# Seven Winograd products of a decoder's mixer in another order, with half of the attention projection split in two

## The chip, the cores and the metric

One NeuronCore of a Trainium2 chip runs the whole program. The metric is the device time of one execution in microseconds; a time of a kernel is the median of several runs.

## What is computed

Two layers, each a mixer and an MLP on 512 tokens of width 1024, all in fp32. The parts that matter here, cut from the reference's description:

```
h = RMSNorm(x)
z = h @ W_in  (columns: attention q k v | mLSTM q k v | mLSTM o-gate | i/f logits | gates A, B)
branch A: causal sliding-window attention (8 heads of 64, window 128)
branch B: mLSTM matrix memory (4 heads), per-head RMS norm, sigmoid output gate
merged = sigmoid(gA) * (A @ W_att_branch) + sigmoid(gB) * (B @ W_m_branch)
x = x + merged @ W_out
x = x + relu(RMSNorm(x) @ W1)^2 @ W2
```

## The kernel before

**Arithmetic.** Each fp32 operand is split into a high and a low part (`split`, `chunk`, `parts_of`: a copy on ScalarE, L165 or L722, then a subtraction on VectorE, L166 or L723), and each product of two blocks is three matmuls (`mm3`, L47): high by high, high by low, low by high. A chunk is 128 rows of a weight, 512 columns wide: loaded into one of three raw buffers, split into one of four pairs of slots.

**What sets the order of a mixer.** The function `mixer` builds a list of steps of matmuls (the *fill*), each 0.25 of a unit, three matmuls; a unit is twelve. Beside it stands a list `side` of functions with a position in units. `weave` (L222) emits the fill in its order and calls each side function when the fill has come to its position. So the order of every engine's queue is written by hand, by these positions; only what stands in `high_priority` or behind `issue_after` is moved.

**The fill before:** the mLSTM q and k (8 units), the gates s0 and s1 (8 each), product 2, the attention branch's projection a in two halves of 512 columns (4 units each, four chunks each, four PSUM banks each), products 5, 1, 3, 6, 7, 4 (2 units each), the gates s2 and s3. There are five banks for all of these.

**The seven products** are a 2 by 2 Winograd form of the product with the columns V and O of W_in. Their second factors are sums of blocks of W_in: products 1 and 2 use a block as it is, through `chunk`; products 5, 6 and 4 use one raw block per k (`wa[k]`, four of them), which is loaded (`begin`, from SP's queue) and gets another block added by a DMA that accumulates (GpSimd's queue, L729); after product 5 has split it another is added (`more`, L717), and after product 6 another. Products 3 and 7 use `wb[k]` (`begin_other`, `more`) in the same way. Product 4 gives its own result, which is added on VectorE (L795) to a copy of product 7's (L793, ScalarE).

**Evacuation of a.** When a half of a is done in its four banks, `ev_a` multiplies each on VectorE with its gate (L915; L910 in the changed file).

**The m phase** (mLSTM) runs as side functions beside s2 and s3: per head `m_decay`, then per block of tokens `m_weights` and `m_out` (four matmuls into an aux bank, then a norm on ScalarE, L892 and L893, and the gate, `m_gate`, on VectorE, L899). After the last one `m_norm` turns the collected squares into factors (two activations with a table load each, L238 and L239, then VectorE L241 to L244), multiplies the four gated rows (L907) and `head_tr` transposes them head by head on TensorE (L52), for the projection of the m branch behind s3. `qk_split` (L674 to L682) readies the mLSTM q and k, with a cast on GpSimd (L676).

Of the kernel before, what the change touches and what calls it, by code (L numbers as in the profile page):

```python
# [12 lines left out]
AF = mybir.ActivationFunctionType  # L13
# [20 lines left out]
def hybrid_kernel(ctx, tc, x, norm_mix, w_in, att_q_norm, att_k_norm, att_sinks, m_gate_bias,  # L34
# [353 lines left out]
    def mixer(l, norm, late, order, phase):  # L388
# [8 lines left out]
        def wcols(c0, n):  # L397
            return lambda k: [W[k * P:(k + 1) * P, c0:c0 + n]]
# [146 lines left out]
        qT, sps, parts = {}, {}, {}  # L545
        tri_i = tri_l.bitcast(I32)

        def k_vec(b):
# [73 lines left out]
        def att_probs(b, kv):  # L622
            sp = sps[b, kv]
            pt = aux()
            for i in range(4):
                pe.transpose(pt[:, i * P:(i + 1) * P], sp[:, i * P:(i + 1) * P], ident)
            hl = split(pt, get=lambda: temp(F32R))
            parts[b, kv] = [(hl, v2[:, 0, max(b - 1, 0), kv])]
            if b > 0:


                own = [temp(F32R) for _ in hl]
                for src, dst in zip(hl, own):
                    s3, d3 = (t.rearrange("p (h q) -> p h q", h=4) for t in (src, dst))
                    gp.affine_select(out=d3, in_=s3, compare_op=ALU.is_ge, fill=0.0, base=0,
                                     pattern=[[0, 4], [1, P]], channel_multiplier=-1)
                parts[b, kv].append((own, v2[:, 1, b - 1, kv]))

        def att_out(b, kv):
# [86 lines left out]
        def begin(k):  # L726
            wa[k] = slot()
            load(wa[k], 0, 0, k)
            gp.dma_start(wa[k], block(0, 1, k), accum_op=ALU.add)  # L729

        def begin_other(k):
            wb[k] = slot()
            load(wb[k], 1, 1, k)
# [55 lines left out]

        def output(t, i, ps, first):  # L790
            if first:
                so.append(slot() if t else temp())
                sc.activation(so[-1], ps, AF.Copy)  # L793
            else:
                ve.tensor_tensor(so[2 * t + i], so[2 * t + i], ps, op=ALU.add)  # L795

        def gates_o():
            for b in range(NB):
                sc.activation(so[b], so[b], AF.Tanh, scale=half[:, b:b + 1])

        plan = {2: ("f", (0, 1), [(output, 0, True)]), 5: ("y", None, [(value, 1, True)]),
                1: ("x", (0, 0), [(output, 0, False)]), 3: ("y", None, [(value, 0, True)]),
                6: ("x", None, [(value, 0, False)]), 7: ("x", None, [(value, 1, False), (output, 1, True)]),
                4: ("f", (1, 1), [(output, 1, False)])}
        held, ready = {}, {}
        by_weights = [(k, i) for k in range(4) for i in range(2)]
        by_tokens = [(2 * h + k, i) for h in range(2) for i in range(2) for k in range(2)]

        def vo_step(n, k, i):
            which, at, outs = plan[n]  # L810
            fresh = n in (5, 1, 2, 4) and k == 0
            if fresh and i == 0:
                held[which] = [bank(), bank()]
            if i == 0:
                ready[k] = weight(n, k)
            wh, wl = ready[k]
            if at:
                c = slice(H * at[0] + i * P, H * at[0] + (i + 1) * P)
                ah, al = (a[:, c] for a in acts[4 * at[1] + k])
            else:  # L820
                ah, al = (a[:, k % 2, i * P:(i + 1) * P] for a in sums[n][k // 2])
            mm3(held[which][i], ah, al, wh, wl, fresh, False, skip_group_check=True)
            if k == 3:
                with tc.high_priority():
                    for f, t, first in outs:
                        f(t, i, held[which][i], first)

        def vo_steps(*ns):
            return [(0.25, lambda n=n, k=k, i=i: vo_step(n, k, i))
                    for n in ns for k, i in (by_tokens if n in (6, 7) else by_weights)]  # L830
# [4 lines left out]
        for i, (b, kv) in enumerate(units):  # L835
# [6 lines left out]
            if kv == 0 and b + 1 < NB:  # L842
                if b + 2 < NB:
                    side += [(at + 1, lambda b=b: k_vec(b + 2)), (at + 1, lambda b=b: q_vec(b + 2))]
                side += [(at + 2 * 1.65 - 1.75, lambda b=b: k_tr(b + 1)), (at + 2 * 1.65 - 2.15, lambda b=b: q_tr(b + 1))]
        side += [(8.45, gating0), (25.5, gating1), (30.5, gating2), (35.5, gating3)]
        side += [(at, lambda m=m, i=i: qk_split(m, i))
                 for at, m, i in ((37.0, 0, 0), (38.0, 2, 0), (39.5, 0, 1), (41.0, 2, 1),
                                  (43.5, 1, 0), (45.0, 3, 0), (46.5, 1, 1), (48.0, 3, 1))]
        g0, s0 = gate_steps(0)  # L850
        g1, s1 = gate_steps(1)

# [29 lines left out]
        def m_out(h, t):  # L882
            ps = aux([P, MV + 1])
            for s in range(t + 1):
                pe.matmul(ps, wts[h, s][:, (t - s) * P:(t - s + 1) * P], vm[0][:, s, h, :],
                          start=s == 0, stop=s == t)
            dn = sm([P, 1], "dn")
            ve.scalar_tensor_tensor(dn, ps[:, MV:], -1.0, em[:, t, h:h + 1], op0=ALU.mult, op1=ALU.max)
            ve.tensor_tensor(dn, ps[:, MV:], dn, op=ALU.max)
            ve.reciprocal(dn, dn)  # L890
            hs = hm[t][:, h * MV:(h + 1) * MV]
            sc.activation(hs, ps[:, :MV], AF.Copy, scale=dn)  # L892
            sc.activation(ps[:, :MV], hs, AF.Square, accum_out=hss[:, t, h:h + 1])  # L893
            if h > 1:
                m_gate(h, t)

        def m_gate(h, t):
            c = slice(h * MV, (h + 1) * MV)
            ve.scalar_tensor_tensor(hm[t][:, c], so[t][:, c], 1.0, hm[t][:, c], op0=ALU.add, op1=ALU.mult)  # L899

        def m_norm():
            ve.tensor_scalar(hss, hss, 1.0 / MV, EPS, op0=ALU.mult, op1=ALU.add)
# [5 lines left out]

        prod = []

        def a_steps(g, sg):
            def ev_a(m, ps):
                t = sg[m]
                prod.append(t)
                ve.scalar_tensor_tensor(t, t, 1.0, ps, op0=ALU.add, op1=ALU.mult)  # L915

            return feat_steps(att_acts, lambda k: [w_att_branch[l, k * P:(k + 1) * P, 512 * g:512 * g + 512]],
                              ev_a)
# [11 lines left out]
        side.append((49.1, gates_o))  # L930
        side += [(49.3 + 0.9 * h + 0.15 * t, lambda h=h, t=t: m_gate(h, t)) for h in range(2) for t in range(NB)]
# [569 lines left out]
```

## Time and profile before

| | |
|---|---|
| median of 3 runs | 1299.78 us (1298.21 to 1300.07) |
| the profiled execution | 1299.13 us |
| its span in the trace | 1297.4 us |
| TensorE | 1282.7 us busy, 99%, 6930 matmuls, clock 1.00 |
| VectorE, ScalarE, GpSimd | 1008.3 us (78%), 776.3 (60%), 236.2 (18%) |
| DMA, mean | 142 GB/s read from HBM over the span |

The first mixer's fill runs from about 61 to 260 us of the span, the second one's some 642 us later. In the rows, PE is TensorE, DVE VectorE, ACT ScalarE, POOL GpSimd, SP the queue that issues most loads. A row of a timeline has its start, its length, engine, line, operation and tiles; the brackets hold the engine's idle time just ahead and what ended it. Matmuls overlap, and their ends are modelled. `x4` is four instructions merged in one row.

### The profile page before, as it was taken

The numbers are of one execution on the slowest core, as the hardware profiler recorded it, in microseconds if no ns is written. First come the engines' busy times: TensorE is split into PE (matmuls) and PEld (weight loads), VectorE is DVE, ScalarE is ACT, GpSimd is POOL, SyncE is SP. The second block draws the span as 40 slices with busy tenths as digits, with TensorE's granted clock in tenths as the row PEclk, the third lists the DMA queues.
The fourth block names the chain that finished last, engine by engine and source line by source line (L and its number), as shares of the span: only waits on it lengthen the run. The fifth ranks groups of instructions, "written<-read, shape, count | busy, mean of one in ns | idle before, by whom it ended". The sixth has DMA issues, their size and how long they took to land.

```text
span 1297.4 us, 19218 instructions
## 1 busy us (share of the span) xinstructions
PE 1282.7 (99%) x6930; PEld 1095.2 (84%) x6930; DVE 1008.3 (78%) x1608; ACT 776.3 (60%) x1367; POOL 236.2 (18%) x313
## 2 busy tenths in 40 slices
PE   9999999999999999999999999999999999999998
PEld 6877778888889999999888777788888899999987
DVE  4688898674777897968958888876747879879797
ACT  5568578553465656656554785775435556665563
POOL 4501252000003021131114023310000030311210
PEclk9999999999999999999999999999999999999999
DMA  5422672272369888898224226722714597988953
GB/s 155 111 74 58 187 130 66 74 243 81 98 163 172 240 183 207 199 206 215 33 77 112 66 60 178 129 77 79 259 50 131 146 214 193 205 210 198 217 142 98
DMA packets 135151, 186.01 MB, mean 143 GB/s; under 512 B 10376, under 2 KB 78832, under 8 KB 135056
## 3 DMA queue, kind: packets, MB, share of 16 engines
q1 hardware_dynamic: 94208, 131.82, 33.2%
q0 software_dynamic: 40128, 52.57, 25.5%
q8 instruction: 54, 0.88, 0.3%
q10 hardware_dynamic: 720, 0.40, 0.1%
q14 instruction: 41, 0.34, 0.1%
HBM read 182.65 MB, written 2.10 MB: 142 GB/s over the span
## 4 chain that ended last, share of the span: by engine, by line
PE 91%; DVE 3%; DMA 3%; ACT 2%; issue 1%; DVEq 0%; SPq 0%; ACTq 0%
PE mm L47 73%; PE aux L47 16%; PE aux L52 2%; DMA w<-in_w_in_dram 2%; DMA w<-in_w_att_branch_dram 1%; ACT wh L165 1%; DVE wl L166 1%; ACT t L615 0%; DVE wl L723 0%; DVE t L583 0%; DVE a L915 0%; DMA x<-in_x_dram 0%; DVE t L620 0%; DVE m L609 0%; DVE t L176 0%
## 5 line engine op out<-in xcount | busy, mean ns | idle before, releaser
L47 PE MATMUL mm<-i,wh 128*128 128x512 f32 (+1 forms) x1280 | 353.9, 363 | 0.2
L992 ACT ACTIVATE wh<-raw 128x1024 fp32r<-128x1024 f32 x212 | 223.3, 1056 | 189.4 <-PE mm L47 118.6
L993 DVE TENSOR_TENSOR wl<-raw,wh 128x1024 fp32r<-128x1024 f32 x212 | 255.1, 1219 | 75.3 <-ACT wh L992 75.3
L47 PEld LDWEIGHTS mm<-i,wh 128*128 128x128 f32 x1280 | 222.7, 189 | 30.7 <-DVE a L695 1.1
L47 PE MATMUL mm<-i,wl 128*128 128x512 f32 (+1 forms) x640 | 228.8, 359 | 0.0
L166 DVE TENSOR_TENSOR wl<-w,wh 128x512 fp32r<-128x512 f32 (+1 forms) x192 | 129.0, 675 | 100.7 <-ACT wh L165 96.3
L165 ACT ACTIVATE wh<-w 128x512 fp32r<-128x512 f32 (+1 forms) x192 | 116.7, 610 | 113.8 <-PE mm L47 85.0
L47 PE MATMUL mm<-wh,uh 128*128 128x512 f32 x440 | 171.8, 390 | 0.0
L47 PE MATMUL mm<-wl,uh 128*128 128x512 f32 x440 | 171.7, 390 | 0.0
L47 PE MATMUL mm<-wh,ul 128*128 128x512 f32 x440 | 171.2, 389 | 0.0
L1152 POOL DMA_DIRECT2D raw<-in_w_ff_dram x48 | 62.2, 1303 | 543.0 <-DVE i L179 234.2
L47 PEld LDWEIGHTS mm<-i,wl 128*128 128x128 f32 x640 | 120.9, 189 | 18.5 <-DVE wl L993 0.4
L47 PE MATMUL mm<-wh,i 128*128 128x512 f32 (+1 forms) x352 | 101.3, 361 | 1.2 <-ACT wh L165 0.6
L1038 DVE SCALAR_TENSOR_TENSOR x<-mm,ms,x 128x512 f32<-128x512 f32 x126 | 90.5, 744 | 9.0 <-PE mm L47 8.9
L47 PEld LDWEIGHTS mm<-wh,ul 128*128 128x128 f32 x440 | 82.6, 188 | 17.5
L47 PEld LDWEIGHTS mm<-wh,uh 128*128 128x128 f32 x440 | 82.8, 188 | 16.1
L47 PEld LDWEIGHTS mm<-wl,uh 128*128 128x128 f32 x440 | 82.8, 188 | 15.6
L47 PE MATMUL mm<-a,wh 128*128 128x512 f32 x256 | 79.8, 393 | 2.3 <-DVE a L915 2.3
L47 PE MATMUL mm<-wh,a 128*128 128x512 f32 x256 | 81.4, 393 | 0.0
L47 PEld LDWEIGHTS mm<-wh,i 128*128 128x128 f32 x352 | 62.0, 188 | 12.4 <-DVE i L179 1.5
L1309 POOL DMA_DIRECT2D raw<-in_w_ff_dram x36 | 43.6, 1212 | 149.2 <-DVE wl L993 103.3
L47 PE MATMUL aux<-t,wh 128*128 128x256 f32 x384 | 69.5, 283 | 0.0
(284 smaller groups left out, 2409.3 us busy)
## 6 DMA issues: line engine op xcount, KB each, us to landing
raw<-in_w_ff_dram SPq DMA_DIRECT2D x144, 512.0 KB, 5.1
raw<-in_w_ff_dram POOLq DMA_DIRECT2D x84, 512.0 KB, 7.9
w<-in_w_in_dram SPq DMA_DIRECT2D x112, 256.0 KB, 2.7
a<-in_w_in_dram POOLq DMA_DIRECT2D x32, 256.0 KB, 5.9
w<-in_w_out_dram SPq DMA_DIRECT2D x32, 256.0 KB, 3.1
w<-in_w_att_branch_dram SPq DMA_DIRECT2D x16, 256.0 KB, 5.4
a<-in_w_in_dram SPq DMA_DIRECT2D x16, 256.0 KB, 5.5
w<-in_w_m_branch_dram SPq DMA_DIRECT2D x16, 256.0 KB, 2.7
```

What stands on the lines that cost most here:

```text
L47: latest[0] = nc.tensor.matmul(*args, **kw)
L52: latest[0] = nc.tensor.transpose(*args)
L165: sc.activation(wh[:, :off], raw[:, :off], AF.Copy)
L166: ve.tensor_tensor(wl[:, :off], raw[:, :off], f32(wh[:, :off]), op=ALU.subtract)
L992: sc.activation(hi, src, AF.Copy)
L993: ve.tensor_tensor(lo, src, f32(hi), op=ALU.subtract)
L1038: ve.scalar_tensor_tensor(xh[:, cc], ps[i][:, cc], ms[j][:, b:b + 1], xh[:, cc], op0=ALU.mult, op1=ALU.add)
L1152: gp.dma_start(to[h], src(h, i, j), accum_op=ALU.add)
L1309: gp.dma_start(to[h], src(h, i, j), accum_op=ALU.add)
```

## The change

The fill becomes: q and k, s0, s1, product 2, the first half of a (4 units, four banks), product 1, the first quarter of a (2 units, two banks), products 5, 6, 3, 7, the second quarter, product 4, s2, s3. Further:

- The eight loads of raw blocks are called at positions 17 to 21.8 where they were at 24.5 to 29.5; the four first accumulations are their own function and are issued behind the last mask of the attention on GpSimd.
- Product 4 goes on in the PSUM banks of products 1, 6 and 7 and gives the sum; its Tanh is taken straight from PSUM. The other gates' Tanh follow their add at once.
- Products 6 and 7 go by weight chunk rather than by pairs of chunks per half of the tokens.
- The m phase, the third gating and the q and k splits start half a unit to a unit and a half later, and the transposes of the heads half a unit; all gates of m are applied where the head's output is.

```diff
@@ vo products @@
         def begin(k):
             wa[k] = slot()
             load(wa[k], 0, 0, k)
-            gp.dma_start(wa[k], block(0, 1, k), accum_op=ALU.add)
+
+        def begin_sum(k):
+            with tc.issue_after(masked[0].ins):
+                gp.dma_start(wa[k], block(0, 1, k), accum_op=ALU.add)
...
             else:
-                ve.tensor_tensor(so[2 * t + i], so[2 * t + i], ps, op=ALU.add)
...
+                ve.tensor_tensor(so[i], so[i], ps, op=ALU.add)
+                sc.activation(so[i], so[i], AF.Tanh, scale=half[:, i:i + 1])
+
+        def output_whole(t, i, ps, first):
+            so.append(slot())
+            sc.activation(so[-1], ps, AF.Tanh, scale=half[:, 2 * t + i:2 * t + i + 1])
...
-        plan = {2: ("f", (0, 1), [(output, 0, True)]), 5: ("y", None, [(value, 1, True)]),
-                1: ("x", (0, 0), [(output, 0, False)]), 3: ("y", None, [(value, 0, True)]),
-                6: ("x", None, [(value, 0, False)]), 7: ("x", None, [(value, 1, False), (output, 1, True)]),
-                4: ("f", (1, 1), [(output, 1, False)])}
+        plan = {2: ("f", (0, 1), [(output, 0, True)]), 1: ("x", (0, 0), [(output, 0, False)]),
+                5: ("y", None, [(value, 1, True)]), 6: ("x", None, [(value, 0, True)]),
+                3: ("y", None, [(value, 0, False)]), 7: ("x", None, [(value, 1, False)]),
+                4: ("x", (1, 1), [(output_whole, 1, True)])}
...
-            fresh = n in (5, 1, 2, 4) and k == 0
+            fresh = n in (5, 1, 2) and k == 0
...
-        side += [(8.45, gating0), (25.5, gating1), (30.5, gating2), (35.5, gating3)]
+        side += [(8.45, gating0), (25.5, gating1), (30.5, gating2), (36.5, gating3)]
...
-                 for at, m, i in ((37.0, 0, 0), (38.0, 2, 0), (39.5, 0, 1), (41.0, 2, 1),
-                                  (43.5, 1, 0), (45.0, 3, 0), (46.5, 1, 1), (48.0, 3, 1))]
+                 for at, m, i in ((38.5, 0, 0), (39.5, 2, 0), (41.0, 0, 1), (42.0, 2, 1),
+                                  (44.5, 1, 0), (45.5, 3, 0), (47.0, 1, 1), (48.0, 3, 1))]
...
+        def a_half_steps(h):
...
+            ps, w = [], []
+
+            def step(q, m, i):
+                if q == 0 and m + i == 0:
+                    ps.extend((bank(), bank()))
+                if m + i == 0:
+                    w[:] = chunk([w_att_branch[l, k * P:(k + 1) * P, 512 + H * h:512 + H * (h + 1)]
+                                  for k in range(2 * q, 2 * q + 2)])
+                k, c = 2 * q + i, slice(H * i + m * P, H * i + (m + 1) * P)
+                mm3(ps[m], w[0][:, c], w[1][:, c], *att_acts[k], k == 0, k == 3)
+                if k == 3:
+                    with tc.high_priority():
+                        ev_a(g1[2 * h + m], ps[m])
...
-        side += [(24.5 + 0.5 * k, lambda k=k: begin(k)) for k in range(4)]
-        side += [(28.0 + 0.5 * k, lambda k=k: begin_other(k)) for k in range(4)]
-        side += [(27.0, sums1), (31.0, lambda: sums_next(6, 0, 0)), (33.5, lambda: sums_next(3, 0, 1)), (38.0, sums3)]
+        side += [(17.0 + 0.6 * k, lambda k=k: begin(k)) for k in range(4)]
+        side += [(20.0 + 0.6 * k, lambda k=k: begin_other(k)) for k in range(4)]
+        side += [(24.6 + 0.3 * k, lambda k=k: begin_sum(k)) for k in range(4)]
+        side += [(27.0, sums1), (31.0, lambda: sums_next(6, 0, 0)), (33.5, lambda: sums_next(3, 0, 1)),
+                 (36.5, sums3)]
...
-            at = 39.6 + pace * h
+            at = 40.6 + pace * h
...
-        side.append((56.9, m_norm))
+        side.append((57.9, m_norm))
...
-        side += [(59.6 + 0.75 * f, lambda f=f: head_tr(f)) for f in range(MH)]
-        weave(feat_steps(acts, wcols(C_QM, 512), ev_qk) + s0 + s1 + vo_steps(2) + a_steps(0, g0) + a_steps(1, g1)
-              + vo_steps(5, 1, 3, 6, 7, 4) + s2 + s3, side)
+        side += [(60.1 + 0.75 * f, lambda f=f: head_tr(f)) for f in range(MH)]
+        weave(feat_steps(acts, wcols(C_QM, 512), ev_qk) + s0 + s1 + vo_steps(2) + a_steps()
+              + vo_steps(1) + a_half_steps(0) + vo_steps(5, 6, 3, 7) + a_half_steps(1) + vo_steps(4)
+              + s2 + s3, side)
```

Three places of the first mixer, in the order of the engines' queues. **SP's queue** around the loads of a's weights (`w<-in_w_att_branch`); the raw blocks are the rows at L713. Before:

```order
L155 DMA w_1805<-in_w_att_branch_dram 128x512
L155 DMA w_1839<-in_w_att_branch_dram 128x512
L713 DMA a_1732<-in_w_in_dram 128x512
L155 DMA w_1859<-in_w_att_branch_dram 128x512
L713 DMA a_1747<-in_w_in_dram 128x512
L713 DMA a_1782<-in_w_in_dram 128x512
L713 DMA a_1801<-in_w_in_dram 128x512
L155 DMA w_1881<-in_w_att_branch_dram 128x512
L155 DMA w_1906<-in_w_att_branch_dram 128x512
L155 DMA w_1951<-in_w_att_branch_dram 128x512
L713 DMA a_1857<-in_w_in_dram 128x512
L713 DMA a_1871<-in_w_in_dram 128x512
```

After, from the last raw block on:

```order
L713 DMA a_1643<-in_w_in_dram 128x512
L155 DMA w_1748<-in_w_in_dram 128x512
L155 DMA w_1762<-in_w_in_dram 128x512
L155 DMA w_1796<-in_w_in_dram 128x512
L155 DMA w_1813<-in_w_att_branch_dram 128x512
L155 DMA w_1847<-in_w_att_branch_dram 128x512
L155 DMA w_1865<-in_w_att_branch_dram 128x512
L155 DMA w_1883<-in_w_att_branch_dram 128x512
L155 DMA w_1907<-in_w_in_dram 128x512
L155 DMA w_1933<-in_w_in_dram 128x512
L155 DMA w_1955<-in_w_in_dram 128x512
L155 DMA w_1967<-in_w_in_dram 128x512
```

All eight raw blocks have left the place among the weights of a, and behind a's first four weights come those of product 1 (`in_w_in`).

**TensorE's queue** at the end of a's first half, before (the first three rows are its last chunk into its fourth bank; `a` as first operand are gated attention rows):

```order
L47 MATMUL mm_1822<-a_635,wh_1883 128x512
L47 MATMUL mm_1822<-a_636,wh_1883 128x512
L47 MATMUL mm_1822<-a_635,wl_1884 128x512
L47 MATMUL mm_1905<-a_629,wh_1908 128x512
L47 MATMUL mm_1905<-a_630,wh_1908 128x512
L47 MATMUL mm_1905<-a_629,wl_1909 128x512
L47 MATMUL mm_1915<-a_629,wh_1908 128x512
L47 MATMUL mm_1915<-a_630,wh_1908 128x512
L47 MATMUL mm_1915<-a_629,wl_1909 128x512
```

After, at the same row numbers:

```order
L47 MATMUL mm_1830<-a_635,wh_1885 128x512
L47 MATMUL mm_1830<-a_636,wh_1885 128x512
L47 MATMUL mm_1830<-a_635,wl_1886 128x512
L47 MATMUL mm_1905<-wh_1909,i_114 128x512
L47 MATMUL mm_1905<-wl_1910,i_114 128x512
L47 MATMUL mm_1905<-wh_1909,i_115 128x512
L47 MATMUL mm_1906<-wh_1909,i_114 128x512
L47 MATMUL mm_1906<-wl_1910,i_114 128x512
L47 MATMUL mm_1906<-wh_1909,i_115 128x512
```

Behind the first half stands product 1 (in its rows the weight stands first and the tokens, `i`, second) with two banks, where the second half of a stood, with four.

**TensorE's queue** at the first head's transposes (L52; `a_170` to `a_173` are the gated rows of the four blocks of tokens, the matmuls around them are s3). Before:

```order
L47 MATMUL mm_2837<-i_274,wh_2970 128x512
L47 MATMUL mm_2837<-i_275,wh_2970 128x512
L47 MATMUL mm_2837<-i_274,wl_2971 128x512
L47 MATMUL mm_2841<-i_274,wh_2970 128x512
L47 MATMUL mm_2841<-i_275,wh_2970 128x512
L47 MATMUL mm_2841<-i_274,wl_2971 128x512
L52 MATMUL aux_2983<-ident,a_170 128x128
L52 MATMUL aux_2983<-ident,a_171 128x128
L52 MATMUL aux_2983<-ident,a_172 128x128
L52 MATMUL aux_2983<-ident,a_173 128x128
L47 MATMUL mm_2855<-i_274,wh_2970 128x512
L47 MATMUL mm_2855<-i_275,wh_2970 128x512
```

After:

```order
L47 MATMUL mm_2834<-i_274,wh_2968 128x512
L47 MATMUL mm_2834<-i_275,wh_2968 128x512
L47 MATMUL mm_2834<-i_274,wl_2969 128x512
L47 MATMUL mm_2796<-i_274,wh_2986 128x512
L47 MATMUL mm_2796<-i_275,wh_2986 128x512
L47 MATMUL mm_2796<-i_274,wl_2987 128x512
L52 MATMUL aux_2993<-ident,a_170 128x128
L52 MATMUL aux_2993<-ident,a_171 128x128
L52 MATMUL aux_2993<-ident,a_172 128x128
L52 MATMUL aux_2993<-ident,a_173 128x128
L47 MATMUL mm_2818<-i_274,wh_2986 128x512
L47 MATMUL mm_2818<-i_275,wh_2986 128x512
```

The transposes stand behind three steps of the chunk before, and behind one now; the last `m_out` (four matmuls at 128x129 into an aux bank) ends 42 matmuls ahead of them before, and 36 after.

More of the change, by code (lines that the diff above doesn't have):

```diff
@@ L544, in mixer @@
         att_acts = [(slot(F32R), slot(F32R)) for _ in range(4)]
-        qT, sps, parts = {}, {}, {}
+        qT, sps, parts, masked = {}, {}, {}, [None]
         tri_i = tri_l.bitcast(I32)
@@ L634, in att_probs @@
                     s3, d3 = (t.rearrange("p (h q) -> p h q", h=4) for t in (src, dst))
-                    gp.affine_select(out=d3, in_=s3, compare_op=ALU.is_ge, fill=0.0, base=0,
-                                     pattern=[[0, 4], [1, P]], channel_multiplier=-1)
+                    masked[0] = gp.affine_select(out=d3, in_=s3, compare_op=ALU.is_ge, fill=0.0, base=0,
+                                                 pattern=[[0, 4], [1, P]], channel_multiplier=-1)
                 parts[b, kv].append((own, v2[:, 1, b - 1, kv]))
@@ L791, in output @@
             if first:
-                so.append(slot() if t else temp())
+                so.append(temp())
                 sc.activation(so[-1], ps, AF.Copy)
             else:
[L795 to L799, printed above, removed]
-        plan = {2: ("f", (0, 1), [(output, 0, True)]), 5: ("y", None, [(value, 1, True)]),
-                1: ("x", (0, 0), [(output, 0, False)]), 3: ("y", None, [(value, 0, True)]),
-                6: ("x", None, [(value, 0, False)]), 7: ("x", None, [(value, 1, False), (output, 1, True)]),
-                4: ("f", (1, 1), [(output, 1, False)])}
+                ve.tensor_tensor(so[i], so[i], ps, op=ALU.add)
[7 more added lines that the diff above has]
+                4: ("x", (1, 1), [(output_whole, 1, True)])}
         held, ready = {}, {}
-        by_weights = [(k, i) for k in range(4) for i in range(2)]
-        by_tokens = [(2 * h + k, i) for h in range(2) for i in range(2) for k in range(2)]
         def vo_step(n, k, i):
             which, at, outs = plan[n]
-            fresh = n in (5, 1, 2, 4) and k == 0
+            fresh = n in (5, 1, 2) and k == 0
             if fresh and i == 0:
@@ L829, in vo_steps @@
             return [(0.25, lambda n=n, k=k, i=i: vo_step(n, k, i))
-                    for n in ns for k, i in (by_tokens if n in (6, 7) else by_weights)]
+                    for n in ns for k in range(4) for i in range(2)]
         units = [(b, kv) for b in range(NB) for kv in range(HKV)]
@@ L893, in m_out @@
             sc.activation(ps[:, :MV], hs, AF.Square, accum_out=hss[:, t, h:h + 1])
[L894 to L899, printed above, removed]
+            ve.scalar_tensor_tensor(hs, so[t][:, h * MV:(h + 1) * MV], 1.0, hs, op0=ALU.add, op1=ALU.mult)
         def m_norm():
@@ L909, in mixer, with ev_a, a_steps @@
         prod = []
[L911 to L918, printed above, removed]
-        side += [(24.5 + 0.5 * k, lambda k=k: begin(k)) for k in range(4)]
-        side += [(28.0 + 0.5 * k, lambda k=k: begin_other(k)) for k in range(4)]
-        side += [(27.0, sums1), (31.0, lambda: sums_next(6, 0, 0)), (33.5, lambda: sums_next(3, 0, 1)), (38.0, sums3)]
+        def ev_a(t, ps):
+            prod.append(t)
+            ve.scalar_tensor_tensor(t, t, 1.0, ps, op0=ALU.add, op1=ALU.mult)
+        def a_steps():
+            return feat_steps(att_acts, lambda k: [w_att_branch[l, k * P:(k + 1) * P, 0:512]],
+                              lambda m, ps: ev_a(g0[m], ps))
+        def a_half_steps(h):
[11 more added lines that the diff above has]
+                        ev_a(g1[2 * h + m], ps[m])
+            return [(0.25, lambda q=q, m=m, i=i: step(q, m, i)) for q in range(2) for m in range(2) for i in range(2)]
+        side += [(17.0 + 0.6 * k, lambda k=k: begin(k)) for k in range(4)]
[3 more added lines that the diff above has]
+                 (36.5, sums3)]
         pace = 3.2
         for h in range(MH):
-            at = 39.6 + pace * h
+            at = 40.6 + pace * h
             side.append((at, lambda h=h: m_decay(h)))
@@ L929, in mixer @@
                          (at + 4.65 + pace * i / NB, lambda h=h, i=i: m_out(h, i))]
-        side.append((49.1, gates_o))
-        side += [(49.3 + 0.9 * h + 0.15 * t, lambda h=h, t=t: m_gate(h, t)) for h in range(2) for t in range(NB)]
-        side.append((56.9, m_norm))
+        side.append((57.9, m_norm))
         g2, s2 = gate_steps(2)
```

## The prediction, made before the changed kernel ran

> **What bounds the kernel now.** I began with the page: busy times, and the shares of the chain that ended last.
>
> ```profile
> span 1297.4 us, 19218 instructions
> PE 1282.7 (99%) x6930; PEld 1095.2 (84%) x6930; DVE 1008.3 (78%) x1608; ACT 776.3 (60%) x1367; POOL 236.2 (18%) x313
> ...
> PE 91%; DVE 3%; DMA 3%; ACT 2%; issue 1%; DVEq 0%; SPq 0%; ACTq 0%
> ```
>
> TensorE has work in flight for 99% of the span, and the chain lies on it for 91%. The matmuls in the file are the same number before and after, so the change can only give or take time in which PE stands still. The waits of PE, longest in total first, are next (in total, times, longest):
>
> ```profile
> PE mm L47 <- DVE a L915: 3.2, 4, 1.4
> ...
> PE mm L47 <- DVE wl L723: 1.0, 2, 0.5
> ...
> PE mm L47 <- DVE wl L166: 0.2, 1, 0.2
> ```
>
> These seven waits, 4.4 us, all lie at the places that the change rewrites; the other waits of that list are at lines it doesn't touch. The timeline of PE shows them one by one, three in the first layer and four in the second (in brackets the idle time ahead and who ended it):
>
> ```profile
> 155.20 0.39 PE L47 MATMUL mm<-a,wl 128*128 128x512 f32 x1
> 156.50 0.73 PE L47 MATMUL mm<-a,wh 128*128 128x512 f32 x2 [0.91 <-DVE a L915]
> ...
> 168.56 0.50 PE L47 MATMUL mm<-wh,t 128*128 128x512 f32 x1 [0.41 <-DVE a L915]
> ...
> 183.04 0.50 PE L47 MATMUL mm<-wl,t 128*128 128x512 f32 x1 [0.47 <-DVE wl L723]
> ...
> 798.67 0.73 PE L47 MATMUL mm<-a,wh 128*128 128x512 f32 x2 [1.40 <-DVE a L915]
> ...
> 810.72 0.50 PE L47 MATMUL mm<-wh,t 128*128 128x512 f32 x1 [0.43 <-DVE a L915]
> ...
> 821.00 0.50 PE L47 MATMUL mm<-wl,i 128*128 128x512 f32 x1 [0.22 <-DVE wl L166]
> ...
> 825.89 0.50 PE L47 MATMUL mm<-wl,t 128*128 128x512 f32 x1 [0.53 <-DVE wl L723]
> ```
>
> A shown gap is less than what is lost: a lone matmul is drawn 0.39 long, while in a full stream the next starts much sooner. The chain gives that pace, in rows that are needed again below:
>
> ```profile
> 245.12 0.89 PE aux L47 x8
> 246.01 9.59 PE mm L47 x42
> 255.60 0.44 PE aux L52 x4
> ```
>
> 9.59 / 42 = 0.228 us from start to start. At 156.50 the loss is 156.50 − 155.20 − 0.23 = 1.07, that is the gap plus 0.16. So the first layer loses 1.07 + 0.57 + 0.63 = 2.27 us, the second 1.56 + 0.59 + 0.38 + 0.69 = 3.22.
>
> Why does PE wait at 156.50? Its next bank is freed by the evacuation of the first half of a, on VectorE, which is behind a weight split, which is behind ScalarE, which is behind a load (timelines of DVE and ACT, then the chain):
>
> ```profile
> 155.16 0.69 DVE L166 TENSOR_TENSOR wl<-w,wh 128x512 fp32r<-128x512 f32 x1 [1.02 <-ACT wh L165]
> 155.77 2.47 DVE L915 SCALAR_TENSOR_TENSOR a<-a,mm 128x512 f32<-128x512 f32 x4
> ...
> 154.49 1.31 ACT L165 ACTIVATE wh<-w 128x512 fp32r<-128x512 f32 x2 [2.58 <-DMA w<-in_w_att_branch_dram]
> ...
> 147.12 7.27 DMA w<-in_w_att_branch_dram
> ```
>
> That load took 7.27 us. The busy time by stages says why: transfers of the raw blocks fill the DMA engines just then (columns: PE, PEld, DVE, ACT, POOL with counts, PE's granted clock, DMA share, GB/s):
>
> ```profile
> 120.00:128.00 8.00, 8.00 (x39) 6.43 (x38) 7.46 (x20) 5.86 (x21) 1.40 (x3) 1.00 0.15 38
> ...
> 142.00:149.00 7.00, 7.00 (x39) 5.82 (x39) 5.23 (x18) 3.39 (x7) 2.60 (x3) 1.00 1.06 257
> ```
>
> **The change part by part.** *Raw blocks sooner.* The eight loads go from the full stretch into one with a DMA share of 0.15, and the four accumulations behind the last mask, before the loads of a. Eight times 256 KB at 257 GB/s is 8 us of transfer that the weights of a no longer wait beside. Nothing on PE needs those blocks until product 5, so I cost the earlier loads at nothing; their cover is that slack, and a load of a weight for s0 or s1 that is delayed among them has two or more chunks of PE work ahead of it. SP now has the loads ahead of those weights, which is the price if the cover fails: some 1 us.
>
> *Order around a.* The first a product hands over to product 1, which needs two banks where the second half of a needed four, and whose weights are early. The evacuation of four banks (2.47 us) stays but nothing stands ahead of it waiting for a load. By hand, with the durations above, it begins as soon as PE ends and its first bank is out about 0.7 us later; product 1 begins in a free bank and wants the next after three matmuls, 0.69. I take the wait as gone (1.07 and 1.56). The half products evacuate two banks, and the first one hands over to product 5 with its weights split before: 0.57 and 0.59 gone. Product 3 no longer comes right behind two adds on VectorE that delayed its split (they end where the split begins):
>
> ```profile
> 181.10 1.27 DVE L795 TENSOR_TENSOR t<-t,mm 128x512 f32<-128x512 f32 x2
> 182.30 1.28 DVE L723 TENSOR_TENSOR wl<-a,wh 128x512 fp32r<-128x512 f32 x2
> ```
>
> So 0.63 and 0.69 go too. The 0.38 at 821.00 I leave in, as it is a split of an ordinary chunk. **Gone: 2.27 + 2.84 = 5.1 us** (bounds 0 and 5.5).
>
> *Product 4 onto the running sum.* Two adds of 0.64 and two copies on ScalarE fall away in each layer; neither engine is the bound, and the row at 181.10 has already been counted. The gates' four Tanh go to where the sums are ready, on a ScalarE that is 60% busy. Nothing.
>
> *The m phase one unit later, its transposes half a unit.* Here the change takes something. The four transposes of the first head need the last gated rows, which come out of a chain from the last m_out (the 8 aux matmuls at 245.12) through ScalarE's two table loads and VectorE's multiplications:
>
> ```profile
> 247.99 1.28 ACT L238 ACT_TABLE_LOAD   x1 [0.49 <-DVE hss L902]
> ...
> 250.03 1.28 ACT L239 ACT_TABLE_LOAD   x1
> ...
> 252.41 0.69 DVE L907 TENSOR_TENSOR a<-a,hr 128x512 f32<-128x512 f32 x1
> 253.02 0.69 DVE L166 TENSOR_TENSOR wl<-w,wh 128x512 fp32r<-128x512 f32 x1
> 253.62 1.89 DVE L907 TENSOR_TENSOR a<-a,hr 128x512 f32<-128x512 f32 x3
> ...
> 255.44 0.60 PE L52 MATMUL aux<-ident,a 128*128 128x128 f32 x4
> ...
> 896.47 1.89 DVE L907 TENSOR_TENSOR a<-a,hr 128x512 f32<-128x512 f32 x3
> ...
> 898.29 0.60 PE L52 MATMUL aux<-ident,a 128*128 128x128 f32 x4
> ```
>
> The last rows are ready at 253.62 + 1.89 = 255.51. By the chain's 0.44 for four, the fourth transpose starts 0.33 behind the first, at 255.77: a slack of 0.26. In the second layer it is 898.36 against 898.62, the same 0.26. Between m_out and the transposes the 42 matmuls become 36 (order below the diff), so PE arrives 6 × 0.228 = 1.37 earlier, and the chain keeps its links. **PE waits 1.37 − 0.26 = 1.11 us in each layer, 2.2 in all** (bounds 0, if the chain runs quicker on less loaded engines, and 2.7). Behind the transposes in PE's queue stands the rest of s3; nobody makes that time good.
>
> *Accumulations into the same block.* Product 6 now follows 5 at once on the same raw blocks, and 7 follows 3. From a chunk of the one to the same chunk of the other were 72 and 48 matmuls; now it is 24, 5.5 us, plus the lead that the four slots for split weights allow, one to three chunks of 1.37. Into that must go the accumulation, a split on ScalarE and one on VectorE. The DMA issues of three windows, 166.4 to 166.7, 150 to 200 and 183.5 to 189.5 us, give the quickest, the middle and the slowest (number, size, median us to landing):
>
> ```profile
> a<-in_w_in_dram POOLq DMA_DIRECT2D x1, 256.0 KB, 4.1
> ...
> a<-in_w_in_dram POOLq DMA_DIRECT2D x12, 256.0 KB, 5.7
> ...
> a<-in_w_in_dram POOLq DMA_DIRECT2D x6, 256.0 KB, 6.1
> ```
>
> 5.7 + 0.63 (an ACT split, as in the 1.31 for two) + 0.68 = 7.0 with no handovers, against 6.9 to 9.6. So at 4.1 nothing is late, and at the median the first chunk waits between 0 and about 0.5 with its handovers; I take 0.2 for each of four places, **0.8 in all** (bounds 0, and what rival 2 gives).
>
> The Trainium skill (DMA: Bandwidth & Descriptors, Anatomy of one DMA — SWDGE (gpsimd) path) fits a transfer that GpSimd issues at about 2.0 us plus its bytes over 436e3. By it 256 KB would land in an estimated 2.6 us, no accumulation here would be late, and the sum would lose its 0.8; the trace does not agree, with a median of 5.7 for these that add into their target.
>
> *GpSimd's casts.* They come behind twelve accumulations now, before among them. With VectorE full one took ten times the other:
>
> ```profile
> 160.37 6.09 POOL L676 CAST a<-a 64x512 fp32r<-64x512 f32 x1 [0.34 <-ACT a L674]
> ...
> 168.21 0.61 POOL L676 CAST a<-a 64x512 fp32r<-64x512 f32 x1
> ```
>
> At 0.61 nobody waits; at 6.09, begun near 182.5 behind the last accumulation, the q block is ready by 188.6, about when PE's first m matmul wants it. I take 0, and 1 us a layer as the upper bound.
>
> **Sum**, against the profiled execution (span 1297.4 and 1.7 around it, 1299.13): 1299.13 − 5.1 + 2.2 + 0.8 = **1297.0 us**. The median of the runs, 1299.78, stands 0.65 above that execution.
>
> **The rivals.** (1) *All gain, no new wait*: the chain ahead of the transposes speeds up with VectorE eased, and the accumulations land in time. 1299.13 − 5.1 = 1294.0. For it: fewer splits and adds in the m phase. Against: the long pieces of the chain are table loads, 2 × 1.28, which no load on other engines explains.
>
> (2) *Late accumulations, slower than before*: products 6 and 7 wait on their raw blocks. At the slowest landing, 6.1, with a lead of one chunk, the first chunk is 6.1 + 1.3 + 0.3 (handovers, an estimate) − 6.9 = 0.8 late, and the other three can add as much again when the landings come slower than one in 1.37: 1.5 a product, 6 in all, 1299.13 − 2.9 + 6 = 1302.2. It decides from 0.73 us a product on (2.9 / 4). For it: a median of 5.7 with fewer in a row. Against: the weights of a are then no longer in the DMA's way, and a lead of three chunks is allowed.
>
> (3) *The waits only move*: the evacuation of each half still stands behind splits, now those of products 1 and 5, and PE waits about as long at the new edges as at the old; the change does not do what it says. With 2.2 at the transposes the 5.1 would have to shrink to about 2.5: 1298.8 to 1299.5. For it: VectorE is as full as before in this stretch. Against: the longest two waits were behind a load, and that load is gone from there.
>
> **How the numbers follow.** The forecast (1296.0 to 1298.5) 0.42; rival 1 0.18; rival 2 0.22; rival 3 0.18. A measurement of this kernel tells about 0.2%, 2.6 us, from no change. Faster by more is under 1296.5: rival 1 and 0.17 of the forecast, 0.35. Slower by more is over 1301.7: 0.14 of rival 2. The rest, 0.51, lies between. The range, 1294.0 to 1302.0, takes in rivals 1 and 3 and most of rival 2.
>
> **What would show it.** Right: no wait of PE for the evacuation of a over 0.2 us, the load of a's weights at 3 to 4 us, and at the first head's transposes a wait of about 1.1 for the gated rows in both layers. Wrong: no wait there (rival 1), waits of PE for the raw blocks' splits near 165 to 180 us (rival 2), or waits for a's halves (rival 3). A PE clock below 1.00 would void all of it.

## The result: 0.6% slower

The changed kernel takes **1306.54 us** (median of 4 runs, 1306.49 to 1307.33), the kernel before 1299.31 (median of 4, 1298.21 to 1300.07): a ratio of 1.0058, 95% interval 1.004 to 1.0075. The forecast was 1297.0, the range 1294.0 to 1302.0. The profiled execution after has a span of 1305.6 us against 1297.4.

The page after, its span, busy times and the shares of the chain:

```profile
span 1305.6 us, 19204 instructions
PE 1285.8 (98%) x6930; PEld 1096.1 (84%) x6930; DVE 1009.5 (77%) x1604; ACT 775.0 (59%) x1363; POOL 226.4 (17%) x313
...
PE 85%; DVE 6%; issue 3%; DMA 3%; ACT 3%; POOL 0%; DVEq 0%; SPq 0%; ACTq 0%; POOLq 0%
```

No engine has more instructions: VectorE and ScalarE have four less each, PE the same 6930. Yet the chain now lies on VectorE for 6% where it was 3%, so PE waits for it more. The waits of PE after (in total, times, longest), those at places of the change and one behind them, at the output projection (L967):

```profile
PE aux L47 <- DVE t L882: 1.9, 2, 1.0
PE aux L52 <- DVE t L474: 1.7, 2, 0.9
PE aux L47 <- ACT aux L895: 1.6, 4, 0.6
...
PE aux L52 <- DVE a L904: 1.1, 4, 0.3
PE mm L47 <- DVE a L910: 0.9, 2, 0.5
...
PE mm L47 <- DVE a L967: 0.8, 1, 0.8
...
PE mm L47 <- ACT t L796: 0.6, 2, 0.4
...
PE mm L47 <- DVE wl L723: 0.2, 1, 0.2
```

Before it was 4.4 us in 7 gaps; now it is 8.8 in 18. With 0.16 hidden in each gap, the growth in this list is 4.4 + 11 × 0.16 = 6.2 of the 8.2 us by which the span grew; the rest is in none of these waits. The first layer's, one by one, in PE's timeline:

```profile
146.01 0.73 PE L47 MATMUL mm<-a,wh 128*128 128x512 f32 x2 [0.26 <-ACT t L796]
156.30 0.50 PE L47 MATMUL mm<-wh,i 128*128 128x512 f32 x1 [0.47 <-DVE a L910]
175.26 0.22 PE L52 MATMUL aux<-ident,t 4*128 4x4 f32 x1 [0.79 <-DVE t L474]
190.25 0.50 PE L47 MATMUL mm<-wl,t 128*128 128x512 f32 x1 [0.20 <-DVE wl L723]
204.97 0.73 PE L47 MATMUL aux<-a,a 128*128 128x512 f32 x2 [0.98 <-DVE t L882]
211.22 0.50 PE L47 MATMUL aux<-cm,sel 128*128 128x512 f32 x1 [0.61 <-ACT aux L895]
218.33 0.73 PE L47 MATMUL aux<-a,a 128*128 128x512 f32 x2 [0.21 <-ACT aux L895]
260.34 0.33 PE L52 MATMUL aux<-ident,a 128*128 128x128 f32 x1 [0.27 <-DVE a L904]
260.94 0.33 PE L52 MATMUL aux<-ident,a 128*128 128x128 f32 x1 [0.27 <-DVE a L904]
...
291.74 0.50 PE L47 MATMUL mm<-wh,a 128*128 128x512 f32 x1 [0.84 <-DVE a L967]
```

From the top: the start of a, the end of its first half, the third gating's transposes, product 7, three places of the m phase, the heads' transposes, and the output projection. What stood behind them follows from the other engines' rows. At the start of a, ScalarE waits for the weight of a's third chunk, with product 2's evacuation (L796) queued behind, and VectorE stands with it:

```profile
144.70 0.63 ACT L165 ACTIVATE wh<-w 128x512 fp32r<-128x512 f32 x1 [3.84 <-DMA w<-in_w_att_branch_dram]
145.36 1.09 ACT L796 ACTIVATE t<-mm 128x512 f32<-128x512 f32 x2
...
145.37 0.69 DVE L166 TENSOR_TENSOR wl<-w,wh 128x512 fp32r<-128x512 f32 x1 [2.97 <-ACT wh L165]
...
155.56 2.48 DVE L910 SCALAR_TENSOR_TENSOR a<-a,mm 128x512 f32<-128x512 f32 x4
```

That load, the third of a's weights in SP's queue (the fourth experiment's text counts it as the second), was issued at 137.7, beside the four first accumulations of 134 us, and took 6.9 us (DMA issues of the windows 137.5 to 137.8 and 134 to 136):

```profile
w<-in_w_att_branch_dram SPq DMA_DIRECT2D x1, 256.0 KB, 6.9
...
a<-in_w_in_dram POOLq DMA_DIRECT2D x4, 256.0 KB, 6.7
```

Behind the 2.97 us VectorE has no pause until it reaches the evacuation at 155.56, too late for PE. Further on, ScalarE waits for an accumulation into product 6's block, and at 182 to 187 both splitting engines stand for product 7's (two rows of ScalarE and one of VectorE, then the busy time of that stretch in the columns of the earlier table):

```profile
171.66 0.63 ACT L722 ACTIVATE wh<-a 128x512 fp32r<-128x512 f32 x1 [1.38 <-DMA a<-in_w_in_dram]
...
183.96 0.63 ACT L722 ACTIVATE wh<-a 128x512 fp32r<-128x512 f32 x1 [2.58 <-PE mm L47]
...
184.63 0.69 DVE L723 TENSOR_TENSOR wl<-a,wh 128x512 fp32r<-128x512 f32 x1 [2.52 <-ACT wh L722]
```

```profile
182.00:187.00 5.00, 5.00 (x23) 3.88 (x22) 1.79 (x4) 2.25 (x4) 1.33 (x2) 1.00 1.03 172
```

The profile puts ScalarE's wait of 2.58 down to a matmul. But the accumulation into this block, issued at 177.60, took 6.3 us and so landed at about 183.9 too; the first experiment below, without it, decides for the accumulation. VectorE works 1.79 us of 5 there, while the DMA engines are full (share 1.03). PE itself waits only 0.2 for product 7: the split weights ahead cover it. But VectorE then has everything still before it, and is full from 187 us into the m phase (15.48 of the 16 us to 203).

### The profile page after: what moved, and what is told of

The parts are those of the page before. It is cut to its first block, busy times and chain, and to the rows that moved or that the text cites. A ratio compares the mean times of both kernels' runs of the same rounds, so it can differ in the third digit from the quotient of the medians.

```text
span 1305.6 us, 19204 instructions
## 1 busy us (share of the span) xinstructions
PE 1285.8 (98%) x6930; PEld 1096.1 (84%) x6930; DVE 1009.5 (77%) x1604; ACT 775.0 (59%) x1363; POOL 226.4 (17%) x313
## 4 chain that ended last, share of the span: by engine, by line
PE 85%; DVE 6%; issue 3%; DMA 3%; ACT 3%; POOL 0%; DVEq 0%; SPq 0%; ACTq 0%; POOLq 0%
PE mm L47 68%; PE aux L47 15%; PE aux L52 2%; DVE wl L166 1%; ACT wh L165 1%; DMA a<-in_w_in_dram 1%; DMA w<-in_w_out_dram 1%; DVE wl L723 1%; DMA w<-in_w_att_branch_dram 1%; ACT t L615 0%; DMA w<-in_w_in_dram 0%; DVE t L583 0%; DVE a L904 0%; ACT t L874 0%; DVE a L967 0%
## 5 line engine op out<-in xcount | busy, mean ns | idle before, releaser
L47 PE MATMUL aux<-i,wh 128*128 128x256 f32 x384 | 69.5, 283 | 0.0
```

The source lines that it names most:

```text
L47: latest[0] = nc.tensor.matmul(*args, **kw)
```

## The experiments

All are timed against the kernel before on the same chip, in five rounds. A gain on the changed kernel is counted from its 1306.54; the kernel before had medians of 1298.97 to 1299.76 beside these runs and 1299.31 beside that one, so a gain of well under 1 us means little.

**Without the later accumulations.**

```diff
         def more(r, i, j, k):
-            with tc.high_priority():
-                gp.dma_start(r, block(i, j, k), accum_op=ALU.add)
+            return
```

> The changed kernel without the accumulations that follow product 5, 6 and 3 (L717); this leaves out the block sums of products 6, 7 and 4, which multiply by the block as the product before left it. Theory A (late accumulations): ScalarE and VectorE stand before the splits of products 6 and 7 until their blocks land, and, as they work in order, the scan of the third gating and the m phase behind them are late. Then the waits of PE for the scan (0.8 and 0.9), for the split of product 7 (0.2) and in the m phase (about 1.8 a layer) go, with the hidden part of each gap some 3.5 us a layer, and the time is about 1299.5. Theory B (the m phase was moved onto the evacuations of the second quarter of a): the waits of the m phase stay, and the time is 1304 or more.

1299.58 us, ratio 1.0005 (0.9997 to 1.0014): 7 us less than the changed kernel. The waits for the scan and for product 7's split are gone, and before product 7's first split VectorE does not stand at all where it stood for 2.52 us; of the m phase's 3.5 in the list 0.7 is left. So the costs at and behind products 6 and 7 come with these transfers, and theory B is out as it was put.

**The heads' transposes half a unit later.**

```diff
-        side += [(60.1 + 0.75 * f, lambda f=f: head_tr(f)) for f in range(MH)]
+        side += [(60.6 + 0.75 * f, lambda f=f: head_tr(f)) for f in range(MH)]
```

> The changed kernel with the transposes of the heads half a unit later, so that 42 matmuls again stand between the last m_out and the first of them. If the wait there is the chain's length against PE's distance, both its gaps (0.27 and 0.27, with the hidden part about 0.9 a layer) go and the time falls by 1.8 to 2.2 us, to about 1304.5. The rival is that the last of the four transposes, now behind the end of s3 by more, makes the m branch's projection wait as long: no change.

1304.34 us, ratio 1.004 (1.0027 to 1.0052): 2.2 less, and PE no longer waits for L904. The forecast's price of this step stands, though the waits for the scan were 1.1 longer in this run's profile.

**Product 4's accumulations behind product 7's.**

```diff
-            if n == 6:
-                more(wa[k], 1, 0, k)
+            if n == 7:
+                with tc.issue_after(masked[0].ins):
+                    gp.dma_start(wa[k], block(1, 0, k), accum_op=ALU.add)
```

(`masked[0]` is then the last accumulation for product 7.)

> The changed kernel with product 4's accumulations behind product 7's in GpSimd's queue instead of ahead of them; same work. Theory A, with the four accumulations of product 4 as what delays those of product 7: the first block of product 7 lands about 2 us sooner, VectorE's wait of 2.5 us before its split shrinks under 1, and the waits of the m phase lose at least half: 1302 to 1304. Theory B: 1306 to 1307, the m phase waits as before.

1304.44 us, ratio 1.0046 (1.0033 to 1.0058), a little above the range expected. VectorE's wait before product 7's split has become shorter:

```profile
184.27 0.69 DVE L723 TENSOR_TENSOR wl<-a,wh 128x512 fp32r<-128x512 f32 x1 [1.58 <-ACT wh L722]
```

It is 1.58, not under 1, and the three waits of the m phase stayed. The queue order on GpSimd is worth at most 2.1 us by the medians, and that is not clear of noise: two of the five runs, 1306.08 and 1307.01, are as long as the changed kernel's. Theory A does not explain the m phase by it.

**Without the first accumulations.**

```diff
         def begin_sum(k):
-            with tc.issue_after(masked[0].ins):
-                gp.dma_start(wa[k], block(0, 1, k), accum_op=ALU.add)
+            return
```

> The changed kernel without the four first accumulations (products 5 and 6 then multiply by one block less in their sums). If these collide with the loads of a's weights, the second weight of a no longer takes 6.9 us, ScalarE's copies of product 2 behind its split are in time, and VectorE is not behind when a's first half ends: the gaps of 0.26 and 0.47 (0.39 and 0.47 in the second layer) go, about 1.0 a layer, time about 1304.3. Rival: the evacuation of a bank is simply longer than the three matmuls that product 1 has without it, so the gap of 0.47 stays and only 0.4 a layer goes, time about 1305.5.

1301.05 us, ratio 1.0016 (1.0006 to 1.0025): 5.5 less, over twice what was expected. The gaps at both ends of a's first half are gone, so they are the collision, not the length of an evacuation; the scan's wait is gone in the first layer and 0.2 in the second, which was not expected.

**The first accumulations held back.**

```diff
-            with tc.issue_after(masked[0].ins):
+            if k == 0:
+                masked[0] = gp.tensor_copy(sm([1, 1], "there", 1), f32(now["wl"])[0:1, 0:1])
+            with tc.issue_after(masked[0].ins):
                 gp.dma_start(wa[k], block(0, 1, k), accum_op=ALU.add)
...
-        side += [(24.6 + 0.3 * k, lambda k=k: begin_sum(k)) for k in range(4)]
+        side += [(28.3, lambda k=k: begin_sum(k)) for k in range(4)]
```

(`now["wl"]` is the split that `chunk` made last.)

> The changed kernel, whole, with its four first accumulations behind a copy of one element of a's third split weight on GpSimd, so that they start near 149 us rather than 134 and no longer run beside the loads of a's weights. If the collision there sets VectorE back for the rest of the stretch, as the run without these accumulations suggests, most of that run's gain comes with no work left out: 1301 to 1302.5, no wait of PE at a's start and end and under 0.3 at the scan. If it was the missing sum work itself that helped (product 5 split sooner), 1305 to 1306.

1302.97 us, ratio 1.003 (1.0018 to 1.0042): 3.6 less with all of the work done, a little above the range expected. The list has no wait at either end of a's first half in either layer; the scan's 0.8 stayed in the first, which was not expected. The accumulations started at 142.6, not near 149. The loads of a's four weights took 2.5 to 3.0 us; two loads of product 1's weights now stand beside the accumulations and take 6.6 and 7.0, but no wait of PE comes of it.

**Three repairs at once** (this one, and the two of the transposes and of product 4).

> The changed kernel with three repairs at once: first accumulations held back as in the run before, transposes half a unit later, product 4's accumulations behind product 7's. If the costs are separate they add up: about 5 + 2 + 2 from 1306.5, that is 1297 to 1298, with the waits of the m phase (about 2 a layer) left. If they share one backlog of VectorE, only 1300 to 1301.

1299.41 us, ratio 1.0004 (0.9995 to 1.0013): 7.1 less, between the two ranges expected; the single gains, 3.6, 2.2 and 2.1, sum to 7.9. They add up nearly, and the waits of the m phase are left. So the whole loss against the kernel before is made good by these three repairs, and what the m phase costs stands against what the change was meant to win.

**The loads alone, in the old order.** The kernel before with `begin` and `begin_other` at 17 to 21.8 and `begin_sum` as in the change.

> The kernel before with the second part of the change alone: loads of the raw blocks at 17 to 21.8, the first accumulations behind the last mask. If the forecast's first term was right where the order is the old one, the wait at the edge of a's halves goes (1.07 and 1.56) and the time falls by 2 to 2.6, to about 1296.7. If the accumulations simply take the loads' place beside a's weights, half of that is given back: 1297.5 to 1299.

1299.28 us, ratio 0.9996 (0.9987 to 1.0005): nothing won. The waits for the evacuation of a are down to 0.9 in each layer, and a wait for L796, 0.4 in each, has come: the accumulations took the loads' place beside a's weights, the third of which took 7.1 us.

**The same with the accumulations held back.**

> The kernel before with early loads and the accumulations held back behind a's third weight. With neither in the way of the first half's weights the edge of a's halves costs nothing: 1296 to 1296.8. The rival is that they now run beside the weights of the second half and only move the wait: 1298 to 1299.5.

1296.33 us, ratio 0.9977 (0.9966 to 0.9987), faster than both kernels, by 3 and 10 us. The waits of PE at the places of the change:

```profile
PE mm L47 <- DVE wl L724: 1.0, 2, 0.5
...
PE mm L47 <- DVE a L921: 0.9, 3, 0.4
...
PE mm L47 <- DVE wl L166: 0.5, 2, 0.2
```

The evacuation of a (L921) costs 0.9 where it was 3.2.

**The m phase later and denser** (on the three repairs).

```diff
-        pace = 3.2
+        pace = 2.95
...
-            at = 40.6 + pace * h
+            at = 41.4 + pace * h
```

> The kernel with the three repairs (held-back accumulations, transposes and product 4's accumulations later), and with the m phase begun 0.8 unit (2.2 us) later but at a pace of 2.95 units a head in place of 3.2, so that it ends at the same place. If the three waits of the m phase (together about 2.2 us a layer, the longest 1.15) are VectorE's backlog behind the late blocks of product 7, which passes, they go: 1299.4 - 4 = about 1295.5. If VectorE is too full in this stretch for the m phase whenever it comes, the waits only move to the next heads: 1298.5 to 1300.

1300.07 us, ratio 1.0005 (0.9996 to 1.0015). The three waits, the first at 203 us, have become one of 1.6 at 211 us and one of 0.3 behind it, in the second layer likewise. They move; a backlog that passes is not the whole of it.

**And the third gating later.**

> The kernel of the run beside it with the third gating a unit later too. Its transposes waited 0.8 for the scan in one layer or both, behind a split that stood for an accumulation. If that is the whole of it, another 0.7 to 1.5 us: 1294.3 to 1295 where the other is 1295.5, and the same distance below it otherwise. If the scan is then late for the m phase's first step, nothing is won.

1300.31 us, ratio 1.0005 (0.9995 to 1.0014). The scan's wait is gone and nothing is won: gaps of 0.2 before splits of products came in the second layer, and the wait of 1.0 at L967's place is in this run and not in the one before.

**The quarters of a together.** When does the m phase get its inputs? The first split of the mLSTM's q and k on ScalarE, before and after:

```profile
159.69 0.61 ACT L674 ACTIVATE a<-a 64x512 fp32r<-64x512 f32 x1
```

```profile
185.78 0.62 ACT L674 ACTIVATE a<-a 64x512 fp32r<-64x512 f32 x1
```

26 us later, though its position moved by 1.5 units (4.1 us). What ScalarE waits for before these splits, in the changed kernel, is VectorE's split of a raw block, the last to read that block's slot (in total, times, longest):

```profile
ACT a L674 <- DVE wl L723: 3.7, 6, 1.2
```

That made theory C.

```diff
-              + vo_steps(1) + a_half_steps(0) + vo_steps(5, 6, 3, 7) + a_half_steps(1) + vo_steps(4)
+              + vo_steps(1) + a_half_steps(0) + a_half_steps(1) + vo_steps(5, 6, 3, 7, 4)
```

> The kernel with the three repairs, and with the second quarter of a right behind the first instead of behind product 7. A new theory C for the waits of the m phase: the attention rows that a multiplies hold eight of the 32 slots until its last quarter is done; in the changed order that is 10 units later, so the q and k splits of the mLSTM find no slot until product 7 has released raw blocks (their first copy on ScalarE starts at 185.8 us, and at 159.7 in the kernel before), and fall on a full VectorE. With the quarters together the slots are free at 36 units, the q and k splits go back to about 160 to 165 us, and the three waits (2.2 a layer) go; product 4 now follows 7 in the same banks and waits for its evacuation, some 0.5 to 0.8 a layer, so 1296 to 1297. If the crowd on VectorE comes from the products' splits and evacuations themselves, the waits stay: 1300 or more.

1305.6 us, ratio 1.0046 (1.003 to 1.0061), with runs from 1301.11 to 1311.29: a miss, and one that does not answer. The splits do go back, to 167.5 us, but product 4's accumulations, behind product 7's, now land (194 to 199 us) when it already wants its blocks; PE waits 1.5 to 2.5 us at the m phase's weights and 1.7 for an evacuation there.

> The run before spoiled its own question: with product 4 right behind product 7, product 4's accumulations behind product 7's landed at 194 to 199 us, after product 4 wanted them. Here the same kernel has them ahead of product 7's again, as in the change; held-back first accumulations, later transposes and the quarters of a together stay. Theory C (slots): the q and k splits run at about 167 to 185 us and the three waits of the m phase are gone or under 0.5 a layer together; against the repairs without this (about 1301 with product 4's accumulations in this place) the time falls by 2 to 4, to 1297 to 1299, less what the casts on GpSimd cost by standing ahead of accumulations. If the m phase's waits stay at about 2 a layer, theory C is wrong: 1301 to 1303.

1299.12 us, ratio 0.9995 (0.9986 to 1.0005), 3.9 below the run with held-back accumulations, from which it differs by the later transposes (2.2) and the quarters (so 1.7 net, just under the 2 to 4 expected). ScalarE's first split and PE's largest wait in this stretch:

```profile
168.28 0.63 ACT L675 ACTIVATE a<-a 64x512 fp32r<-64x512 f32 x1 [1.36 <-PE mm L47]
...
198.81 0.47 PE L47 MATMUL mm<-wh,i 128*128 128x512 f32 x1 [0.92 <-DVE vm L794]
```

The waits at m's weights and aux banks are gone in both layers. In their place PE waits 0.92 for product 7's evacuation, since product 4 follows it in the same banks. This is what theory C expected, and the first split now waits for a matmul (1.36 us), no longer for the split of a raw block. One thing is not separated: this order also takes the last quarter's own splits and evacuation away from the start of the m phase. That these alone do not make the waits is shown by the first experiment, where they stayed and 0.7 of 3.5 was left; there the first split of q and k came at 182.6, 3.2 us sooner than in the changed kernel, once the raw blocks were free sooner.

## Why the prediction was wrong

**What bounds it: right.** No engine's work decided, but where PE stands still: each run that was clearly quicker than the changed kernel lacks some of its waits.

**"Raw blocks sooner ... I cost the earlier loads at nothing": this step failed.** The loads were free; the accumulations that went with them were not. The text put them "behind the last mask, before the loads of a" and counted only what they left. They land at 138.6 to 144.4 us, over the load of a's third weight, which took 6.9 us in place of the forecast 3 to 4. Loads alone in the old order won nothing, held-back accumulations won 3.0 there and 3.6 in the new order, so the collision is shown.

**Order around a, 5.1 us gone: mis-sized.** The edges of a's first half cost 0.47 + 0.16 and 0.26 + 0.16 in the first layer, 1.05 where 2.27 was (with 0.36 more for product 7), and 1.18 where 2.84 was counted. The first-half edge stayed because VectorE was behind from 145 us on; without the collision it vanished in both layers.

**The transposes: right.** Forecast 2.2; taking the wait away gave 2.2. The two gaps in each layer are 0.60 from start to start where 0.11 is usual, 0.98 in all, against 1.11.

**Accumulations into the same block, 0.8: the place was right, the way to PE was not.** PE's own wait for a raw block is 0.2. But the splits for products 6 and 7 stand in the same queues as all else on ScalarE and VectorE, and for 1.4 and 2.5 us those engines did nothing (1.79 of 5 us busy). The scan for the gating behind them was then 0.79 late, which the forecast did not price at all. The landing taken, 5.7, was about right: they take 4.3 to 6.3 here. The Trainium skill's fit (DMA: Bandwidth & Descriptors, Anatomy of one DMA — SWDGE (gpsimd) path) gives an estimated 2.6 for 256 KB, and the trace does not agree for transfers that add.

**"At 0.61 nobody waits" for the m phase, at most 1 us a layer: this failed too, and not by the cast.** All casts took 0.61, also where VectorE was busy for 15.48 of 16 us (187 to 203), so a full VectorE alone does not make them slow. But the q and k splits ahead of them started 26 us late. The attention rows that a multiplies stay in eight slots until its last quarter; and the end of a was moved from unit 34 to 44. The q and k splits got slots only from product 7's raw blocks, whose release hung on the late accumulations. That fits the run without these, in which the m phase was eased too. The waits there come to about 2.2 us a layer, the largest term that the forecast lacked.

**Rival 2** named the place and a price of 6, and 1302.2; it had 0.22. It too looked for the wait on PE at the raw blocks, and the time lies above it as well.

**The sum by measured terms:** −1.2 and −1.7 at the edges of a and product 3's split, −0.4 for the gap at 821.00, which is gone too, +2.0 transposes, +2.0 scan (two gaps of 0.8 and 0.9 with what they hide), +0.4 product 7, +4.5 m phase, +1.0 at L967, is +6.6 of 8.2. The remaining 1.6 is not placed. Open stays the L967 term: one wait of 0.8 to 1.0 at the output projection, beside a slow load of W_out (ScalarE waited 2.09 us for it in the changed kernel), is in some of these runs and not in others. The profiled runs without the later accumulations, without the first ones, with product 4's later and with the first ones held back do not have it, so up to 1 us of what each of them gained may be this wait.

## What to carry to other kernels

An accumulating DMA takes bandwidth from its neighbours like a load (the load of a's third weight took 6.9 us beside four of them and 2.5 with them held back); moving "the loads" means to find a place for both, beside loads that can afford to be late. Where one engine splits, evacuates and feeds several phases in order, a wait that is covered for PE still stops everything behind it; price it at the engine's next deadline, not at the tile's own reader. And a step that is moved later holds its operands' buffers longer: ask who was going to get them.

## What the runs showed of the hardware

With the DMA engines full (share 1.03 to 1.06), plain loads beside accumulations moved 257 GB/s (142 to 149 us before), accumulations alone 172 GB/s (182 to 187 us after). At about the same share of the DMA engines, the blocks that are added moved fewer bytes a second.
